# A tuned trunk kernel whose first projection block does without GpSimd's tensor arithmetic

## Chip, cores and metric

The kernel runs on one core of one Trainium2 chip. The metric is the device time of one launch in microseconds (us), of which the median of the runs is taken. The engines of the core are named as the profile names them: PE (TensorE, the matrix multiplier), DVE (VectorE), ACT (ScalarE), POOL (GpSimd) and SP (SyncE, which issues transfers). Every engine takes its instructions in the order in which they were written; engines wait for one another by semaphores.

## What is computed

The reference is a trunk of two layers on x (1 x 1024 x 1024, float32): a causal spatial-gating layer, then a Mamba-2 layer, each behind an RMSNorm. All that the change touches lies at the very start, in the norm and the first of three column groups of `h @ w_in`:

```python
def rmsnorm(x, w):
    xf = x.astype(jnp.float32)
    y = xf * lax.rsqrt(jnp.mean(xf * xf, axis=-1, keepdims=True) + NORM_EPS)
    return (y * w.astype(jnp.float32)).astype(x.dtype)

def spatial_gating_mixer(h, w_in, ln_w, ln_b, w_s, b_s, w_out):
    z, u, v = jnp.split(h @ w_in, 3, axis=-1)
    v = layernorm(v, ln_w, ln_b)
    ...
    return (u * mixed * jax.nn.silu(z)) @ w_out

h = h + spatial_gating_mixer(rmsnorm(h, norm_w), ...)
```

The columns of `v` are computed first, 512 at a time; `head()` computes the first 512 of them (block 0 of `v_block`), together with the norm and the transposes of x.

## The kernel before

**One block.** A block multiplies the normalized rows (1024 tokens x 1024) by 1024 x 512 weights. It cuts both into halves and uses seven products instead of eight. Of the rows, A11 and A12 are the first 512 tokens (first and second half of the contraction), A21 and A22 the other 512. Of the weights, b11, b12, b21, b22 are 512 x 256 each; they are loaded by SP into four slots `wr`. The sums are S1 = A21 + A22, S2 = S1 - A11, S3 = A11 - A21, S4 = A12 - S2 for the rows, and t1 = b12 - b11, t2 = b22 - t1, b21 - t2 and b22 - b12 for the weights. Product 1 takes A11, 2 takes A12, 3 takes S4, 4 takes A22, 5 takes S1, 6 takes S2, 7 takes S3.

**Two parts of each number.** Every operand is split into a rounded part and the rest (`hi` on ACT, then `lo` on DVE; names `hh`, `hl` for rows, `wh`, `wl` for weights). A product is then three matmuls: `wh*hh` (L134), `wl*hh` (L135), `wh*hl` (L136). One product is 48 matmuls of 128x256.

**The head's order.** `head()` is a schedule written out by hand. Rows come in eight tiles of 128 tokens, rows 0 to 3 for A11/A12, rows 4 to 7 for A21/A22. For each tile: the squares' sum (`sq`, ACT, L361), 1/sqrt in two parts (`rs_a`: DVE L365 and POOL's power L141; `rs_b`: four DVE operations on 128x2, L150 to L153), the scaling (`norm`, DVE, L376, two halves), eight transposes on PE (`tr`, L382), then copies back (`copy`, ACT, L398; the tile then holds the transposed row, F[t], in two halves) and the split (`hi` L391, `lo` L395). PE does products 1 and 2 half by half as rows come in, then 4 (with the transposes of rows 6 and 7 in between), 6, 7, 5, 3, and then product 1 of the next block (`nxt.mm(1)`).

**Who makes the sums.** POOL makes t1, t2 (L452, L453), b21 - t2 and b22 - b12 (L459, L460), S3 (L413), S1 of rows 4 to 6 (L416), the rest of two weights (`ylo`, L405) and S4 of rows 5 to 7 (L422). S4 needs A12 again, whose place was reused; `again` (L410) rebuilds it from its two parts. DVE makes S1 of row 7, S2 (L419) and S4 of row 4. In the trace the tile names are those of the program: `xp` holds rows 0 to 3, `xrow` rows 4 to 6, and row 7 lies in a slot `wr`, which it shares in turn with the weights; so `wr<-wr 128x512` is S1 of row 7. The junk output of the squares goes into the room of S4's split (`hh`, `hl`).

**The next block's weights** are loaded by SP (L120) into the same four `wr` slots, as each comes free. Stores of v go to `v_d` (L335).

Of the kernel before, what the change touches and what calls it, by code (L numbers as in the profile page):

```python
# [22 lines left out]
G = 8  # L23
# [6 lines left out]
def kernel(  # L30
# [49 lines left out]
    def wr(shape, name="wr"):  # L80
        return sb.tile(shape, F32, name=name, tag="wr", bufs=4)
# [90 lines left out]
    def new_H(names):  # L172
        return {n: (s8([P, 4, 512], "hh", F32R), s8([P, 4, 512], "hl", F32R)) for n in names}
# [3 lines left out]

    nwb = [k2([P, 512], "nwb") for _ in range(2)]
    xr = x.rearrange("(c p) d -> c p d", p=P)
    HS = new_H(("A11", "A12", "A22", "S1", "S2", "S3", "S4"))  # L180

    class Block:

# [103 lines left out]
        def post(self, n, i, parts=(0, 1)):  # L287
            a = self.acc[n][i]
            if n in (1, 6, 7) and 0 in parts:
                if i == 0:  # L290
                    self.u[n] = q4([P, 2, 512], "u")
                nc.scalar.copy(out=self.u[n][:, i], in_=a)  # L292
            if n == 2:
                self.done("C11", i, a, self.u[1][:, i])
            elif n == 4 and a is self.acc[1][i]:
                self.done("C21", i, a, None)
            elif n == 7 and 1 in parts and 4 in self.acc:
                self.done("C21", i, self.acc[4][i], self.u[7][:, i])
# [23 lines left out]
    def v_block(gp):  # L322
# [17 lines left out]

        return Block(HS, W, True, done)

    prow, prow2 = k1([P, P], "prow"), k1([P, P], "prow2")

    def head():

        blk = v_block(0)
        V, S, G = nc.vector, nc.scalar, nc.gpsimd
        TTv, TTg = V.tensor_tensor, G.tensor_tensor
        rows, F, TP, ss, rs = {}, {}, {}, {}, {}  # L350

        def load_x(t, dst):
            nc.sync.dma_start(out=dst, in_=xr[t])
            rows[t] = dst
            F[t] = dst.rearrange("p (h k t) -> p h k t", h=2, k=4)

        def sq(t):
            if t % 2 == 0:
                ss[t] = tiny([P, 8], "ss")
            junk = HS["S4"][t // 2 % 2][:, t % 2 * 2:t % 2 * 2 + 2].rearrange("p a b -> p (a b)")  # L360
            S.activation(junk, rows[t], AF.Square, accum_out=ss[t // 2 * 2][:, t % 2:t % 2 + 1])  # L361

        def rs_a(t):
            v = ss[t][:, 0:2]
            V.tensor_scalar(v, v, 1.0 / D, NORM_EPS, ALU.mult, ALU.add)  # L365
            ss[t + 1] = rsqrt_a(v, 2)

        def rs_b(t):
            r = tiny([P, 8], "rs")
            rsqrt_b(r[:, 0:2], ss[t][:, 0:2], ss[t + 1], 2)  # L370
            rs[t], rs[t + 1] = r[:, 0:1], r[:, 1:2]

        def norm(t):
            for kh in (0, 1) if t < 4 else (1, 0):
                xh = rows[t][:, kh * 512:(kh + 1) * 512]
                V.scalar_tensor_tensor(xh, xh, rs[t], nwb[kh], ALU.mult, ALU.mult)  # L376

        def tr(t):
            tp = [(sm if t in (0, 3, 5, 7) else acc)("tp") for _ in range(2)]
            for kh in (0, 1) if t < 4 else (1, 0):  # L380
                for k in range(4):
                    nc.tensor.transpose(out=tp[kh][:, k * P:(k + 1) * P],  # L382
                                        in_=rows[t][:, (kh * 4 + k) * P:(kh * 4 + k + 1) * P], identity=ident)
            TP[t] = [a.rearrange("p (k t) -> p k t", k=4) for a in tp]

        def part(name, t):
            sl = slice(t % 4 * P, (t % 4 + 1) * P)
            return [m[:, :, sl] for m in HS[name]]

        def hi(name, t, src):  # L390
            S.copy(out=part(name, t)[0], in_=src)  # L391

        def lo(name, t, src):
            h_, l_ = part(name, t)
            TTv(out=l_, in0=src, in1=h_.bitcast(F32), op=ALU.subtract)  # L395

        def copy(t, kh):
            S.copy(out=F[t][:, kh], in_=TP[t][kh])  # L398

        def yhi(n, src, eng=S.copy):  # L400
            blk.Y[n] = (wh([P, 4, 256]), wl([P, 4, 256]))
            eng(out=blk.Y[n][0], in_=src)
# [4 lines left out]
        def again(t):

            h_, l_ = part("A12", t)
            TTg(out=F[t][:, 1], in0=h_.bitcast(F32), in1=l_.bitcast(F32), op=ALU.add)  # L410

        def s3(t):
            TTg(out=F[t - 4][:, 0], in0=F[t - 4][:, 0], in1=F[t][:, 0], op=ALU.subtract)  # L413

        def s1(t, eng):
            eng(out=F[t][:, 0], in0=F[t][:, 0], in1=F[t][:, 1], op=ALU.add)  # L416

        def s2(t):
            TTv(out=F[t][:, 1], in0=F[t][:, 1], in1=F[t - 4][:, 0], op=ALU.subtract)  # L419

        def s4(t, eng=TTg):
            eng(out=F[t - 4][:, 1], in0=F[t - 4][:, 1], in1=F[t][:, 1], op=ALU.subtract)  # L422
# [11 lines left out]
        for kh, j in ((0, 0), (1, 0), (0, 1), (1, 1)):  # L434
            blk.load(kh, j)
        for t in range(4, 8):
            load_x(t, q4([P, D], "xrow") if t < 7 else wr([P, D]))

        nc.sync.dma_start(out=prow, in_=b_conv_w[0].rearrange("k (c p) -> (k c) p", p=P))
        for o, ap in ((0, a_ln_w), (16, a_ln_b), (32, b_norm_w), (48, b_conv_b)):  # L440
            n = ap.shape[1] // P
# [10 lines left out]
        TTg(out=t1, in0=b[0, 1], in1=b[0, 0], op=ALU.subtract)  # L452
# [28 lines left out]
        blk.mm(4, 1, False)
        yhi(7, b[0, 1]), ylo(7, b[0, 1], TTg)
        for t in (4, 5):
            s2(t), hi("S2", t, F[t][:, 1])
        for t in (4, 5):
            lo("S2", t, F[t][:, 1])
        s2(6), hi("S2", 6, F[6][:, 1]), s1(7, TTv), s2(7), hi("S2", 7, F[7][:, 1])
        for t in (6, 7):
            lo("S2", t, F[t][:, 1])
        for t in range(4):  # L490
            again(t)
# [8 lines left out]
        ylo(5, t1, TTg)  # L500
        s4(4, TTv)
        for t in range(5, 8):
            s4(t)
# [100 lines left out]
    for g in range(G):  # L604
# [41 lines left out]
        blk = Block(HS, lambda kh, j: [a_w_in[kh * 512:(kh + 1) * 512, j * DI + g * 256:j * DI + (g + 1) * 256]],  # L646
                    False, done_zu)
# [555 lines left out]
    V = nc.vector  # L1203
# [760 lines left out]
```

## Time and profile before

| | us |
|---|---|
| median of 3 runs (1590.07 to 1592.04) | 1591.79 |
| the profiled execution | 1599.45 |
| its span (first to last instruction) | 1597.6 |
| busy in the span: PE / DVE / ACT / POOL | 1503.3 / 1063.6 / 782.9 / 420.2 |
| granted TensorE clock, mean | 0.975 |

The span's 40 slices are 40 us each; in the first one PE is busy five tenths of the time, in the second seven tenths, and in nearly all others nine. The head is the first 92 us. A row of the timeline reads: start, duration, engine, line, operation, output and input tiles with their shape and type, count, and in brackets how long the engine stood idle ahead of it and for whom. A row with a count over 1 is a run of equal instructions with their total time.

### The profile page before, as it was taken

To read this page: it belongs to the slowest core of one execution; us is meant where nothing else is said; L and a number is where in the kernel's file an instruction comes from. 1 tells how busy PE (TensorE), PEld (TensorE's weight loads), DVE (VectorE), ACT (ScalarE), POOL (GpSimd) and SP (SyncE) were. 2 spreads that over 40 slices of the span, in tenths; PEclk is the share of its full clock that TensorE was granted. 3 is DMA by queue.
4 is the path that set the end of the run, shared out by engine and by line. 5 is a ranking of instruction groups with operands and counts; after the bars stand their busy time and mean duration, and the time that the engine had idled before them with its cause. 6 is when DMAs were issued, how large, how long until landed. Compare 5 with 4: busy or idle time off the path is not lost.

```text
span 1597.6 us, 21214 instructions
## 1 busy us (share of the span) xinstructions
PE 1503.3 (94%) x7830; PEld 1239.6 (78%) x7830; DVE 1063.6 (67%) x1701; ACT 782.9 (49%) x1251; POOL 420.2 (26%) x441
## 2 busy tenths in 40 slices
PE   5799999999999999998999999989999999987997
PEld 4799988888888887776788787767777777766876
DVE  7976566666666644777737377646776666777876
ACT  4522232332323354655555555546666666755363
POOL 3601110000000131210011312116766666532121
PEclk8899999999999999999999999999999999998999
DMA  5154323322333999856367878666566464677872
GB/s 174 41 174 143 106 98 111 111 98 98 110 110 111 329 262 245 191 128 139 99 159 178 165 165 158 162 188 188 162 180 179 133 183 126 198 270 167 221 139 105
DMA packets 174839, 251.82 MB, mean 158 GB/s; under 512 B 16288, under 2 KB 102928, under 8 KB 171536
## 3 DMA queue, kind: packets, MB, share of 16 engines
q1 hardware_dynamic: 124120, 168.39, 33.9%
q0 software_dynamic: 39520, 63.19, 20.5%
q10 hardware_dynamic: 11096, 18.90, 3.3%
q8 instruction: 62, 1.02, 0.3%
q14 instruction: 41, 0.34, 0.1%
HBM read 185.61 MB, written 51.18 MB: 148 GB/s over the span
## 4 chain that ended last, share of the span: by engine, by line
PE 59%; issue 15%; DVE 10%; ACT 7%; DMA 6%; POOL 1%; SPq 1%; ACTq 1%; POOLq 0%; DVEq 0%
PE acc L136 10%; PE acc L134 9%; PE acc L135 9%; PE ab L134 4%; PE ab L136 4%; PE ab L135 4%; PE yy L1571 2%; PE yy L1575 2%; DVE wl L112 2%; PE bo L135 2%; PE bo L134 2%; PE bo L136 2%; PE ao L134 2%; PE ao L135 2%; PE ao L136 2%
## 5 line engine op out<-in xcount | busy, mean ns | idle before, releaser
L134 PE MATMUL acc<-hh,wh 128*128 128x512 f32 x868 | 343.2, 395 | 15.0 <-ACT u L292 7.2
L136 PE MATMUL acc<-hh,wl 128*128 128x512 f32 x868 | 341.7, 394 | 2.2 <-DVE wl L112 2.1
L135 PE MATMUL acc<-hl,wh 128*128 128x512 f32 x868 | 340.2, 392 | 0.0
L134 PEld LDWEIGHTS acc<-hh,wh 128*128 128x128 f32 x868 | 164.6, 190 | 51.9 <-ACT u L292 8.9
L112 DVE TENSOR_TENSOR wl<-wr,wh 128x1024 fp32r<-128x1024 f32 (+1 forms) x97 | 115.6, 1193 | 125.8 <-ACT wh L111 125.8
L136 PEld LDWEIGHTS acc<-hh,wl 128*128 128x128 f32 x868 | 164.5, 189 | 39.9 <-DVE wl L112 5.5
L135 PEld LDWEIGHTS acc<-hl,wh 128*128 128x128 f32 x868 | 164.5, 190 | 33.4
L111 ACT CAST wh<-wr 128x1024 fp32r<-128x1024 f32 (+1 forms) x113 | 116.5, 1031 | 103.1 <-PE acc L135 56.7
L292 ACT COPY u<-acc 128x512 f32<-128x512 f32 x117 | 67.7, 583 | 200.1 <-PE acc L136 198.5
L136 PE MATMUL acc<-wh,hl 128*128 128x256 f32 x448 | 131.7, 294 | 12.4 <-DVE hl L395 12.4
L134 PE MATMUL ab<-hh,wh 128*128 128x512 f32 x288 | 129.5, 450 | 7.2 <-DVE x L1281 3.8
L134 PE MATMUL acc<-wh,hh 128*128 128x256 f32 x448 | 132.5, 296 | 3.8 <-DVE vt L331 2.1
L135 PE MATMUL acc<-wl,hh 128*128 128x256 f32 x448 | 130.9, 292 | 1.3 <-DVE wl L405 1.3
L135 PE MATMUL ab<-hl,wh 128*128 128x512 f32 x288 | 114.3, 397 | 3.2 <-DVE hl L112 3.2
L136 PE MATMUL ab<-hh,wl 128*128 128x512 f32 x288 | 115.2, 400 | 0.0
L136 PEld LDWEIGHTS acc<-wh,hl 128*128 128x128 f32 x448 | 90.2, 201 | 13.5 <-DVE hl L395 13.5
L134 PEld LDWEIGHTS acc<-wh,hh 128*128 128x128 f32 x448 | 90.4, 202 | 4.8 <-ACT wh L111 2.3
L135 PEld LDWEIGHTS acc<-wl,hh 128*128 128x128 f32 x448 | 90.5, 202 | 1.7 <-DVE wl L405 1.5
L134 PE MATMUL bo<-wh,xh 128*128 128x512 f32 x192 | 78.5, 409 | 8.0 <-ACT wh L111 7.2
L112 DVE TENSOR_TENSOR xl<-ya,xh 128x1024 fp32r<-128x1024 f32 x40 | 49.9, 1246 | 53.1 <-ACT xh L111 53.1
L1544 ACT ACTIVATE wl<-wl,tk 128x128 f32<-128x128 f32 x256 | 81.5, 391 | 0.6 <-DMA wl<-cs_d 0.3
L645 POOL DMA_DIRECT2D y_d<-y x8 | 4.4, 548 | 290.9 <-DVE y L642 290.9
(320 smaller groups left out, 3284.0 us busy)
## 6 DMA issues: line engine op xcount, KB each, us to landing
wr<-in_a_w_in_dram SPq DMA_DIRECT2D x48, 512.0 KB, 3.8
wl<-cs_d SPq DMA_DIRECT2D x64, 256.0 KB, 3.4
wr<-in_b_w_in_dram SPq DMA_DIRECT2D x30, 512.0 KB, 5.1
wb<-in_a_w_out_dram SPq DMA_DIRECT2D x10, 1024.0 KB, 11.2
wb<-in_b_w_out_dram SPq DMA_DIRECT2D x10, 1024.0 KB, 8.0
wr<-in_b_w_in_dram SPq DMA_DIRECT2D x36, 256.0 KB, 5.7
v<-v_d SPq DMA_DIRECT2D x8, 1024.0 KB, 5.0
y_d<-y POOLq DMA_DIRECT2D x8, 1024.0 KB, 5.6
```

Of the source, the lines that this page charges most:

```text
L111: nc.scalar.copy(out=hi, in_=src)
L112: return (eng or nc.vector).tensor_tensor(out=lo, in0=src, in1=hi.bitcast(F32), op=ALU.subtract)
L134: nc.tensor.matmul(out=o, lhsT=l[0], rhs=r[0], start=start, stop=False, **kw)
L135: nc.tensor.matmul(out=o, lhsT=l[0], rhs=r[1], start=False, stop=False, **kw)
L136: nc.tensor.matmul(out=o, lhsT=l[1], rhs=r[0], start=False, stop=stop, **kw)
L292: nc.scalar.copy(out=self.u[n][:, i], in_=a)
L645: store = lambda: nc.gpsimd.dma_start(out=y_d[-1], in_=y)
L1544: nc.scalar.activation(wl[:, j, :], wl[:, j, :], AF.Relu, scale=-1.0, bias=tokc(2, c, self.g)[:, j:j + 1])
L1571: nc.tensor.matmul(out=yy[f * 64:(f + 1) * 64, pt * P:(pt + 1) * P], lhsT=w[:, j * 64:(j + 1) * 64], rhs=wl[:, j, :], start=True, stop=True)
L1575: nc.tensor.matmul(out=yy[:, 256 + pt * P:384 + pt * P], lhsT=self.state[c - 1][:, pt * P:(pt + 1) * P], rhs=self.x(3, c), start=True, sto ...
```

## The change

POOL's tensor operations leave the head, except for the four tiny powers (L141); what they did goes to DVE, to ACT, or to transfers that add to their destination (`accum_op=ALU.add`).

- `copy` of rows 4 to 7 now multiplies by -1 (ACT), so the tiles hold -A21 and -A22, and every row sum becomes an addition: S3 = A11 + (-A21), -S1, -S2, and S4 = A12 + (-S2). `hi` and `lo` put the sign right for S1 and S2.
- The adds of S3 and S2, and of S1 for rows 6 and 7, are DVE's. S1 of rows 4 and 5 and all of S4 are adding transfers from tile to tile, issued by POOL.
- t1, t2 and b21 - t2 are DVE's. b22 - b12 is a multiplication by -1 on ACT and an adding transfer from memory (`add`, L202).
- A12 is kept by four more copies on ACT; `again` is gone. The rests of two weights (`ylo` 7 and 5) go from POOL to DVE.
- Row 7 goes into a `q4` tile like rows 4 to 6. The squares' junk and product 1's stored accumulator (`u[1]`) share a new tile `side`; the room of S4's split is taken only when it is needed.

```diff
         def hi(name, t, src):
-            S.copy(out=part(name, t)[0], in_=src)
+            h_ = part(name, t)[0]
+            if name in MINUS:
+                S.mul(h_, src, -1.0)
+            else:
+                S.copy(out=h_, in_=src)
...
         def copy(t, kh):
-            S.copy(out=F[t][:, kh], in_=TP[t][kh])
+
+            if t < 4:
+                S.copy(out=F[t][:, kh], in_=TP[t][kh])
+            else:
+                S.mul(F[t][:, kh], TP[t][kh], -1.0)
...
+        def sums(eng, *names):
+
+            for n, t in names:
+                a, c = {3: (F[t - 4][:, 0], F[t][:, 0]), 1: (F[t][:, 0], F[t][:, 1]),
+                        2: (F[t][:, 1], F[t - 4][:, 0]), 4: (F[t - 4][:, 1], F[t][:, 1])}[n]
+                if eng is None:
+                    nc.gpsimd.dma_start(out=a, in_=c, accum_op=ALU.add)
+                else:
+                    eng.tensor_tensor(out=a, in0=a, in1=c, op=ALU.add)
...
-            load_x(t, q4([P, D], "xrow") if t < 7 else wr([P, D]))
+            load_x(t, q4([P, D], "xrow"))
...
-        TTg(out=t1, in0=b[0, 1], in1=b[0, 0], op=ALU.subtract)
-        TTg(out=t2, in0=b[1, 1], in1=t1, op=ALU.subtract)
         blk.mm(1, 0, False), sq(4), blk.post(1, 0), sq(5)
         blk.mm(2, 0, False)
         norm(2), tr(2), norm(3), tr(3)
-        rs_a(4), rs_b(4), norm(4)
...
-        TTg(out=b[1, 0], in0=b[1, 0], in1=t2, op=ALU.subtract)
-        TTg(out=b[0, 1], in0=b[1, 1], in1=b[0, 1], op=ALU.subtract)
...
+        rs_a(4)
+        TTv(out=t1, in0=b[0, 1], in1=b[0, 0], op=ALU.subtract)
+        rs_b(4), norm(4)
...
         norm(5)
+        TTv(out=t2, in0=b[1, 1], in1=t1, op=ALU.subtract)
+        TTv(out=b[1, 0], in0=b[1, 0], in1=t2, op=ALU.subtract)
...
-        for t in (4, 5):
-            s3(t), s1(t, TTg)
-        yhi(6, t2)
+        sums(V, (3, 4), (3, 5)), sums(None, (1, 4), (1, 5))
+        S.mul(b[0, 1], b[0, 1], -1.0), blk.add(b[0, 1], 1, 1), yhi(6, t2)
...
-        s3(6), s1(6, TTg), s3(7)
+        sums(V, (2, 4), (2, 5), (3, 6), (1, 6))
         blk.mm(4, 1, False)
...
+            hi("S2", t, F[t][:, 1]), lo("S2", t, F[t][:, 1])
+        sums(V, (3, 7), (1, 7), (2, 7), (2, 6)), sums(None, (4, 4), (4, 5))
+        for t in (7, 6):
+            hi("S2", t, F[t][:, 1]), lo("S2", t, F[t][:, 1])
+        yhi(7, b[0, 1]), ylo(7, b[0, 1])
+        sums(None, (4, 6), (4, 7))
```

What this moves is seen best in the order of the instructions. First DVE between the squares of rows 4 and 5 and the rests of A11 and A12 of rows 2 and 3, before (L365 and L150 to L153 are the 1/sqrt, L376 the scaling, L395 the rests, L405 the rest of b21 - t2):

```order
L365 TENSOR_SCALAR ss<-ss 128x2
L150 TENSOR_TENSOR ru<-rr 128x2
L151 TENSOR_TENSOR ru<-ru,ss 128x2
L152 TENSOR_SCALAR ru<-ru 128x2
L153 TENSOR_TENSOR rs<-rr,ru 128x2
L376 SCALAR_TENSOR_TENSOR xrow<-xrow,rs,nwb 128x512 x2
L395 TENSOR_TENSOR hl<-tp,hh 128x4x128 x4
L376 SCALAR_TENSOR_TENSOR xrow<-xrow,rs,nwb 128x512 x2
L405 TENSOR_TENSOR wl<-wr,wh 128x1024
```

The same place in the changed kernel (`t_104` is t1, `t_105` is t2; the lines are 364, 375, 401 and 415 there, L598 is another part's tiny operation):

```order
L364 TENSOR_SCALAR ss<-ss 128x2
L461 TENSOR_TENSOR t_104<-wr 128x1024
L150 TENSOR_TENSOR ru<-rr 128x2
L151 TENSOR_TENSOR ru<-ru,ss 128x2
L152 TENSOR_SCALAR ru<-ru 128x2
L153 TENSOR_TENSOR rs<-rr,ru 128x2
L375 SCALAR_TENSOR_TENSOR xrow<-xrow,rs,nwb 128x512 x2
L401 TENSOR_TENSOR hl<-tp,hh 128x4x128 x4
L375 SCALAR_TENSOR_TENSOR xrow<-xrow,rs,nwb 128x512 x2
L467 TENSOR_TENSOR t_105<-wr,t_104 128x1024
L598 TENSOR_SCALAR hv<-hv 128x1
L468 TENSOR_TENSOR wr<-wr,t_105 128x1024
```

Three weight sums of 128x1024 came in: one between L364 and the 1/sqrt, two ahead of the rest of b21 - t2.

The second place is DVE at S2, the operand of product 6. Before (L405 the rest of t2, L395 the rests, L419 the S2 of rows 4, 5, 6 and 7, `wr<-wr` S1 of row 7):

```order
L405 TENSOR_TENSOR wl<-t_107,wh 128x1024
L395 TENSOR_TENSOR hl<-tp,hh 128x4x128 [waits PE_49,Activation_49]
L419 TENSOR_TENSOR xrow<-xrow,xp 128x512 [waits Pool_49] x2
L395 TENSOR_TENSOR hl<-xrow,hh 128x4x128 [waits Activation_49] x2
L419 TENSOR_TENSOR xrow<-xrow,xp 128x512 [waits Pool_49]
L416 TENSOR_TENSOR wr<-wr 128x512 [waits PE_49,Pool_49]
L419 TENSOR_TENSOR wr<-wr,xp 128x512 [waits DVE_49]
```

In the changed kernel (`xrow<-xrow,xp` is S2, `xp<-xp,xrow` S3, `xrow<-xrow` S1; a name that begins with DMASW is the semaphore of a POOL queue transfer):

```order
L415 TENSOR_TENSOR wl<-t_105,wh 128x1024
L401 TENSOR_TENSOR hl<-tp,hh 128x4x128 [waits PE_49,Activation_49]
L425 TENSOR_TENSOR xrow<-xrow,xp 128x512 [waits DMASW0_49]
L425 TENSOR_TENSOR xrow<-xrow,xp 128x512 [waits DMASW1_49]
L425 TENSOR_TENSOR xp<-xp,xrow 128x512
L425 TENSOR_TENSOR xrow<-xrow 128x512 [waits DVE_49]
L399 SCALAR_TENSOR_TENSOR hl<-xrow,hh 128x4x128 [waits Activation_49] x2
L425 TENSOR_TENSOR xp<-xp,xrow 128x512
L425 TENSOR_TENSOR xrow<-xrow 128x512 [waits DVE_49,PE_49]
```

S2 of rows 4 and 5 waited for POOL's S3 and S1; now it waits for the adding transfers of S1, which read the same half that S2 then overwrites, and S3 and S1 of row 6 stand behind it.

The third place is POOL's queue after the last power (L423 the adding transfers: `xrow<-xrow` S1 of rows 4 and 5, `xp<-xrow` S4; L202 adds b22 to -b12; L335 stores v):

```order
L423 DMA xrow<-xrow 128x512 [waits DMAHW2_49,DVE_49,Activation_49]
L423 DMA xrow<-xrow 128x512 [waits DMAHW3_49,DVE_49]
L202 DMA wr<-in_a_w_in_dram 128x4x256 [waits Activation_49]
L423 DMA xp<-xrow 128x512 [waits DMAHW0_49,DVE_49]
L423 DMA xp<-xrow 128x512 [waits DMAHW1_49,DVE_49]
L423 DMA xp<-xrow 128x512 [waits DMAHW4_49,DVE_49]
L423 DMA xp<-xrow 128x512 [waits DMAHW5_49]
L335 DMA v_d_93<-vt 128x512 [waits DVE_49]
```

In this stretch POOL held 16 tensor operations before; now it only issues seven adding transfers. From the first product of the next block on, the order is the same on every engine.

More of the change, by code (lines that the diff above doesn't have):

```diff
@@ L179 @@
     xr = x.rearrange("(c p) d -> c p d", p=P)
-    HS = new_H(("A11", "A12", "A22", "S1", "S2", "S3", "S4"))
+    HS = new_H(("A11", "A12", "A22", "S1", "S2", "S3"))
     class Block:
@@ L289, in post @@
             if n in (1, 6, 7) and 0 in parts:
-                if i == 0:
+                if i == 0 and n not in self.u:
                     self.u[n] = q4([P, 2, 512], "u")
@@ L347, in head @@
         blk = v_block(0)
-        V, S, G = nc.vector, nc.scalar, nc.gpsimd
-        TTv, TTg = V.tensor_tensor, G.tensor_tensor
+        V, S = nc.vector, nc.scalar
+        TTv, MINUS = V.tensor_tensor, ("S1", "S2")
         rows, F, TP, ss, rs = {}, {}, {}, {}, {}
@@ L359, in sq @@
                 ss[t] = tiny([P, 8], "ss")
-            junk = HS["S4"][t // 2 % 2][:, t % 2 * 2:t % 2 * 2 + 2].rearrange("p a b -> p (a b)")
-            S.activation(junk, rows[t], AF.Square, accum_out=ss[t // 2 * 2][:, t % 2:t % 2 + 1])
+            S.activation(side[:, 0], rows[t], AF.Square, accum_out=ss[t // 2 * 2][:, t % 2:t % 2 + 1])
         def rs_a(t):
@@ L390, in hi @@
         def hi(name, t, src):
-            S.copy(out=part(name, t)[0], in_=src)
+            h_ = part(name, t)[0]
[3 more added lines that the diff above has]
+                S.copy(out=h_, in_=src)
         def lo(name, t, src):
             h_, l_ = part(name, t)
-            TTv(out=l_, in0=src, in1=h_.bitcast(F32), op=ALU.subtract)
+            if name in MINUS:
+                V.scalar_tensor_tensor(l_, src, -1.0, h_.bitcast(F32), ALU.mult, ALU.subtract)
+            else:
+                TTv(out=l_, in0=src, in1=h_.bitcast(F32), op=ALU.subtract)
         def copy(t, kh):
-            S.copy(out=F[t][:, kh], in_=TP[t][kh])
+            if t < 4:
+                S.copy(out=F[t][:, kh], in_=TP[t][kh])
+            else:
+                S.mul(F[t][:, kh], TP[t][kh], -1.0)
         def yhi(n, src, eng=S.copy):
@@ L405, in ylo @@
             eng(out=blk.Y[n][1], in0=src, in1=blk.Y[n][0].bitcast(F32), op=ALU.subtract)
[L407 to L422, printed above, removed]
+        def sums(eng, *names):
[4 more added lines that the diff above has]
+                    nc.gpsimd.dma_start(out=a, in_=c, accum_op=ALU.add)
+                else:
+                    eng.tensor_tensor(out=a, in0=a, in1=c, op=ALU.add)
         b = blk.b
@@ L426, in head @@
         blk.t1, blk.t2 = t1, t2
+        side = s8([P, 2, 1024], "side")
+        blk.u[1] = side[:, 1].rearrange("p (i n) -> p i n", i=2)
         xp = [s8([P, 2, D], "xp") for _ in range(2)]
@@ L445, in head @@
         norm(0), tr(0), norm(1), tr(1)
-        hi("A11", 0, TP[0][0]), copy(0, 0), sq(3), hi("A12", 0, TP[0][1])
+        hi("A11", 0, TP[0][0]), copy(0, 0), sq(3), hi("A12", 0, TP[0][1]), copy(0, 1)
         rs_a(2), yhi(1, b[0, 0], V.tensor_copy)
         lo("A11", 0, TP[0][0]), ylo(1, b[0, 0]), lo("A12", 0, TP[0][1]), rs_b(2)
-        hi("A11", 1, TP[1][0]), copy(1, 0), hi("A12", 1, TP[1][1])
+        hi("A11", 1, TP[1][0]), copy(1, 0), hi("A12", 1, TP[1][1]), copy(1, 1)
         lo("A11", 1, TP[1][0]), lo("A12", 1, TP[1][1])
         yhi(2, b[1, 0]), ylo(2, b[1, 0])
-        TTg(out=t1, in0=b[0, 1], in1=b[0, 0], op=ALU.subtract)
-        TTg(out=t2, in0=b[1, 1], in1=t1, op=ALU.subtract)
         blk.mm(1, 0, False), sq(4), blk.post(1, 0), sq(5)
@@ L456, in head @@
         norm(2), tr(2), norm(3), tr(3)
-        rs_a(4), rs_b(4), norm(4)
-        hi("A11", 2, TP[2][0]), copy(2, 0), hi("A12", 2, TP[2][1])
-        TTg(out=b[1, 0], in0=b[1, 0], in1=t2, op=ALU.subtract)
-        TTg(out=b[0, 1], in0=b[1, 1], in1=b[0, 1], op=ALU.subtract)
-        lo("A11", 2, TP[2][0]), lo("A12", 2, TP[2][1])
-        hi("A11", 3, TP[3][0]), copy(3, 0), hi("A12", 3, TP[3][1])
-        lo("A11", 3, TP[3][0]), lo("A12", 3, TP[3][1])
+        rs_a(4)
+        TTv(out=t1, in0=b[0, 1], in1=b[0, 0], op=ALU.subtract)
+        rs_b(4), norm(4)
+        for t in (2, 3):
+            hi("A11", t, TP[t][0]), copy(t, 0), hi("A12", t, TP[t][1]), copy(t, 1)
+            lo("A11", t, TP[t][0]), lo("A12", t, TP[t][1])
         norm(5)
+        TTv(out=t2, in0=b[1, 1], in1=t1, op=ALU.subtract)
+        TTv(out=b[1, 0], in0=b[1, 0], in1=t2, op=ALU.subtract)
         blk.mm(1, 1, False, (0,)), tr(4), blk.mm(1, 1, False, (1,))
@@ L479, in head @@
         lo("A22", 7, TP[7][1])
-        s3(6), s1(6, TTg), s3(7)
+        sums(V, (2, 4), (2, 5), (3, 6), (1, 6))
         blk.mm(4, 1, False)
-        yhi(7, b[0, 1]), ylo(7, b[0, 1], TTg)
         for t in (4, 5):
[L484 to L491, printed above, removed]
+            hi("S2", t, F[t][:, 1]), lo("S2", t, F[t][:, 1])
[4 more added lines that the diff above has]
+        sums(None, (4, 6), (4, 7))
         for i in range(2):
@@ L499, in head @@
             lo("S3", t, F[t - 4][:, 0])
[L500 to L503, printed above, removed]
+        ylo(5, t1)
         for i in range(2):
@@ L516, in head @@
             nxt.load(kh, j)
+        HS.update(new_H(("S4",)))
         for t in range(4, 8):
```

## Prediction

> **What bounds the kernel now.** The page's slices point at the first 90 us, so I read stretches of it first (columns: length, busy time of PE, its weight loads, DVE, ACT and POOL, granted clock, DMA share, GB/s).
>
> ```profile
> 20.00:60.00 40.00, 27.48 (x182) 26.49 (x182) 37.01 (x47) 18.47 (x36) 21.06 (x15) 0.83 0.18 50
> 60.00:92.00 32.00, 27.77 (x190) 27.40 (x191) 29.42 (x36) 13.61 (x22) 12.34 (x7) 0.84 0.22 77
> 92.00:112.00 20.00, 20.00 (x169) 20.00 (x168) 14.10 (x20) 6.23 (x8) 1.34 (x2) 1.00 0.74 222
> ```
>
> From 20 to 60 us DVE works 37 of 40 us and everybody waits for it. From 92 us PE never stops: a head that ends earlier hands its gain to PE whole. So the head's end, the first matmul of the next block's product 1 at 92.08, is what to move. PE's timeline shows the waits on the way:
>
> ```profile
> 22.13 0.58 PE L136 MATMUL acc<-wh,hl 128*128 128x256 f32 x1 [3.13 <-DVE hl L395]
> 34.49 0.58 PE L136 MATMUL acc<-wh,hl 128*128 128x256 f32 x1 [3.85 <-DVE hl L395]
> 47.70 1.94 PE L382 MATMUL tp<-ident,xrow 128*128 128x128 f32 x8 [2.97 <-issue]
> 60.36 0.39 PE L136 MATMUL acc<-wh,hl 128*128 128x256 f32 x1 [3.28 <-DVE hl L395]
> 66.76 0.39 PE L136 MATMUL acc<-wh,hl 128*128 128x256 f32 x1 [1.74 <-DVE hl L395]
> 84.77 0.36 PE L134 MATMUL acc<-wh,hh 128*128 128x256 f32 x1 [2.12 <-DVE vt L331]
> 92.08 0.28 PE L134 MATMUL acc<-wh,hh 128*128 128x256 f32 x1
> ```
>
> Nearly all name DVE's rests. A wait also costs clock, as the same view of shorter stretches shows:
>
> ```profile
> 68.10:71.30 3.20, 3.20 (x17) 3.20 (x17) 2.79 (x5) 1.70 (x5) 0.00 (x0) 0.50 0.00 0
> 85.20:88.40 3.20, 3.20 (x17) 3.20 (x16) 3.17 (x6) 0.00 (x0) 0.00 (x0) 0.50 0.50 187
> 88.80:92.00 3.20, 3.20 (x29) 3.20 (x28) 3.17 (x7) 0.00 (x0) 0.00 (x0) 1.00 0.44 164
> ```
>
> After the waits at 66.76 and 84.77 the granted clock is 0.50 for a while: 17 matmuls in 3.2 us where there are 29 at full clock. Such a stretch loses 12/29 of 3.2, and with its edges about 1.4 us.
>
> Why is DVE late? Its timeline beside POOL's:
>
> ```profile
> 7.96 0.16 DVE L150 TENSOR_TENSOR ru<-rr 128x2 f32<-128x2 f32 x1 [0.83 <-POOL rr L141]
> 8.76 2.74 DVE L376 SCALAR_TENSOR_TENSOR xp<-xp,rs,nwb 128x512 f32<-128x512 f32 x4
> 16.44 2.37 POOL L452 TENSOR_TENSOR t<-wr 128x1024 f32<-128x1024 f32 x1 [1.36 <-DMA wr<-in_a_w_in_dram]
> 16.77 2.06 DVE L150 TENSOR_TENSOR ru<-rr 128x2 f32<-128x2 f32 x1
> 21.38 1.29 DVE L395 TENSOR_TENSOR hl<-tp,hh 128x512 fp32r<-128x512 f32 x2
> 27.34 2.33 DVE L150 TENSOR_TENSOR ru<-rr 128x2 f32<-128x2 f32 x1 [0.81 <-POOL rr L141]
> 32.42 1.42 DVE L376 SCALAR_TENSOR_TENSOR xrow<-xrow,rs,nwb 128x512 f32<-128x512 f32 x2
> ```
>
> An operation on 128x2 takes 0.16 us at 7.96 and 2.06 at 16.77, ending at 18.83, just when POOL's L452 ends (18.81). I read it so that a POOL tensor operation holds such a DVE operation until it is done. This is what the change takes away.
>
> **The change part by part.** The sum follows the chain to 92.08.
>
> *Up to 22.13.* The four operations of the 1/sqrt take 0.80 us (7.96 to 8.76) when POOL is idle, and 4.61 here (16.77 to 21.38): 3.8 less. Two more copies on ACT (0.6 each) now stand ahead of the halves that DVE reads here; I keep **3.5**.
>
> *22.13 to 34.49.* The same four go from 5.08 (27.34 to 32.42) to 0.8: 4.3 less. Among them now stands the sum t1 on DVE. Its price:
>
> ```profile
> 96.62 1.22 DVE L260 TENSOR_TENSOR wr<-wr 128x1024 f32<-128x1024 f32 x1
> 97.76 1.21 DVE L225 TENSOR_TENSOR wr<-wr,t 128x1024 f32<-128x1024 f32 x1
> ```
>
> One after the other they cost 1.14 each, of which 0.81 falls into the idle time ahead of 27.34. Net **4.0**.
>
> *34.49 to 47.70.* Here the change costs: two more sums on DVE (2.3) now stand ahead of ACT's rounding of b21 - t2, and behind that, on ACT, stand two halves of row 4 and the squares of rows 6 and 7. The prices on ACT and the places on DVE:
>
> ```profile
> 43.37 1.08 ACT L402 CAST wh<-t 128x1024 fp32r<-128x1024 f32 x1
> 39.72 1.06 ACT L361 ACTIVATE hl<-wr 128x1024 fp32r<-128x1024 f32 x1
> 40.90 0.17 DVE L365 TENSOR_SCALAR ss<-ss 128x2 f32<-128x2 f32 x1 [1.39 <-ACT hl L361]
> 42.37 0.77 DVE L150 TENSOR_TENSOR ru<-rr 128x2 f32<-128x2 f32 x1
> 45.65 0.68 DVE L395 TENSOR_TENSOR hl<-tp,hh 128x512 fp32r<-128x512 f32 x1
> 46.25 2.00 DVE L376 SCALAR_TENSOR_TENSOR xrow<-xrow,rs,nwb 128x512 f32<-128x512 f32 x2
> ```
>
> With 7.5 gained, DVE comes to the rests of rows 2 and 3 at 26.2 (32.42 and 1.3 for two scalings, less 7.5). From there: four rests 2.6, two scalings 1.4, two sums 2.3, ACT's rounding 1.1, two halves 1.2 and two squares of 1.2 with their readout bring the next L365 to 37.2, against 40.90 before: only 3.7 of the 7.5 are left there. From there on it wins again: the four tiny operations take 3.28 (42.37 to 45.65) and will take 0.8, two scalings 2.00 against 1.42.
>
> 3.7 + 2.5 + 0.6 = 6.8, so the term is **-0.7**: row 6's transposes move from 47.70 to about 40.9.
>
> *47.70 to 60.36, the new wait.* DVE's S2:
>
> ```profile
> 54.71 3.92 DVE L419 TENSOR_TENSOR xrow<-xrow,xp 128x512 f32<-128x512 f32 x2
> 58.56 3.44 DVE L395 TENSOR_TENSOR hl<-xrow,hh 128x512 fp32r<-128x512 f32 x2
> 61.93 1.76 DVE L419 TENSOR_TENSOR xrow<-xrow,xp 128x512 f32<-128x512 f32 x1
> 63.61 1.76 DVE L416 TENSOR_TENSOR wr<-wr 128x512 f32<-128x512 f32 x1
> ```
>
> Undisturbed one costs 0.65 (the two rests at 21.38). The two S2 save 2.7, the first rest 1.1, the rest of t2 ahead of them another 1.1. Added: S3 of rows 4 and 5 (1.2), and S3 and S1 of row 6 ahead of the rests (1.3). What is left hangs on the S1 transfers of 256 KB, which POOL issues when S3 of rows 4 and 5 and the scaled halves are there, at about 43.7 and 44.5. No transfer of before is one from tile to tile at this place. The nearest are L745's adding ones:
>
> ```profile
> ya<-ya POOLq DMA_DIRECT2D x12, 512.0 KB, 15.4
> L745 POOL DMA_DIRECT2D u<-h_d x1: 865/865/865, 1497.7 to 1497.7; - x1
> DMA to landing us min/median/max: 5.0/5.0/5.0
> DMA to landing us min/median/max: 4.5/11.0/23.5
> ```
>
> The second and third rows are one 256 KB transfer that was first in its queue, 5.0 us; the last row is all of L745, 4.5 to 23.5, most of them queued behind others. Here POOL's queue is empty, so I take 5.0, with the second 1.5 later: 48.7 and 50.2. DVE reaches S2 at about 47.9, so it stands 0.8 and then some 0.9. Sum: -4.9 + 2.5 + 1.7 = **0.7** gained; both ends of the landing (4.5 and 23.5) are kept for the range.
>
> The Trainium skill, "DMA: Bandwidth & Descriptors", section "Anatomy of one DMA — SWDGE (gpsimd) path", fits 2.0 us plus the bytes at 436 GB/s; by it 256 KB would land in an estimated 2.6 us, DVE would not wait, and some 1.5 us more would be gained. The lone row says 5.0 and decides.
>
> *60.36 to 66.76.* Three operations of 1.76 (the rest, S2 and S1) become 0.6 each, but one S3 comes in: the rests of rows 6 and 7 are done 1.5 sooner than this stretch took: **1.5**.
>
> *66.76 to 84.77.* DVE's rests of S1, and with them product 5 and the accumulator at 84.77:
>
> ```profile
> 72.90 5.88 DVE L395 TENSOR_TENSOR hl<-xrow,hh 128x512 fp32r<-128x512 f32 x3 [2.01 <-ACT hh L391]
> 78.70 1.78 DVE L395 TENSOR_TENSOR hl<-wr,hh 128x512 fp32r<-128x512 f32 x1
> ```
>
> Four rests take 7.66 beside POOL, and 2.6 without it; against these 5.1 stand two rests of weights (2.3) that come to DVE, while one S4 add (0.7) leaves. DVE gets some 3.5 us of air, and the wait of 2.12 at 84.77 goes; next late would be the S4 transfers, issued by about 57 and needed at about 69. With PE fed after 66.8, the slow matmuls of 68 to 71 go as well (1.4): **3.5**.
>
> *84.77 to 92.08.* No wait, so no slow stretch from 85.2: **1.4**.
>
> At nothing: ACT's multiplication by -1 costs what a copy costs (two rows below, 627 and 595 ns), and ACT is busy only 18.5 of the 40 us from 20 on. Row 7's load, the squares' place and S4's room free nothing that a wait names. SP's next weights go out earlier, since a `wr` slot is free; beside the S1 transfers two of them may cost up to 3 us, which the range takes in.
>
> ```profile
> L217 ACT ACTIVATE t<-wr 128x512 f32<-128x512 f32 x1 | 0.6, 627 | 0.0
> L398 ACT COPY xrow<-tp 128x512 f32<-128x512 f32 x6 | 3.3, 595 | 0.0
> ```
>
> **Sum:** 3.5 + 4.0 - 0.7 + 0.7 + 1.5 + 3.5 + 1.4 = 13.9 us: 92.08 becomes 78.2, and the profiled 1599.45 (its span of 1597.6 and 1.85 around it, which nothing touches) becomes 1585.5. The profiled execution is 7.7 longer than the median 1591.79; the head is a fixed piece of both, so the median becomes **1577.9**.
>
> **Rivals.**
>
> *The transfers land late.* For it: all of L745 have a median of 11.0, and two SP loads run beside. Each microsecond over 5.0 holds S2 and all DVE work behind it as long. 7 to 12 us cost 2 to 7: 1580 to 1585.
>
> The Trainium skill, "SBUF — State Buffer", section "SBUF: two separate sides", says that such transfers starve while DVE runs an operation that uses both of its ports, since POOL can't write their descriptors. By it they would land only in DVE's pauses, which the first S2 would make itself. POOL's issue of the lone row, 865 ns, shows no such stall, but not with DVE at work as densely as here.
>
> *The waits come back.* DVE has seven operations more between 42 and 70 us (four S3, one S1, two rests of weights); if the waits at 66.76 and 84.77 stay with their slow stretches, 3.5 and 1.4 fall away: 13.9 - 4.9 = 9.0, so 1582.8.
>
> *Slower.* The transfers take what `ya<-ya` takes, median 15.4. With a landing of L, S2 is L - 5.0 later, and so are the last S4 adds, issued at 57 + (L - 5.0) and landing L + 1.3 after that: at 53.3 + 2L. Product 3 needs them; its 48 matmuls (5.3 to 5.8 us at full clock, by 29 in 3.2 and a few lost records) and a slow stretch (1.4) put the next block at 60.5 + 2L. It decides from L = 15.8 (92.08); with 20 the head ends at 100.5, 8.4 late: 1592 to 1600. Against it: those rows are twice as large and stand in a queue of their own kind.
>
> *It doesn't do what it says:* DVE's long operations are not POOL's doing. Then DVE keeps them and carries some 8 us of added work (three sums and two rests of weights at 1.14, five row sums at 0.65, less one S4): slower, 1592 to 1600. Against it stand the common ends at 18.8.
>
> **How the numbers follow.** A measurement tells about 0.2% (3 us) from no change. Forecast 0.76 (1574.5 to 1580.5: slow stretches ±1.4, latencies ±0.7, a landing of 4.5 to 6), late transfers 0.12, waits back 0.06, slower 0.03, POOL not the cause 0.03. The range 1573.5 to 1585 takes in the first three. A partial loss that ends within 3 us of before is about 0.03, cut from the second and third: faster 0.91, same 0.03, slower 0.06.
>
> **What would show it.** Tiny operations of 0.16 us at 17 and 24 us; row 6's transposes near 41; DVE waiting for a transfer ahead of the first S2 at about 48, under 1.5 us; no wait of PE for `vt` near 72; the next block's L134 at 78 ± 3. Wrong it would be if the S1 rows show landings over 10 us, or if PE of the next block, which now starts earlier, waits for its weights.

## The result and the profile after

| | before | after |
|---|---|---|
| median, us | 1591.91 (4 runs, 1590.07 to 1596.3) | 1581.48 (4 runs, 1579.54 to 1582.27) |
| the profiled execution, its span | 1599.45, 1597.6 | 1582.27, 1580.5 |
| head's end (first matmul of the next block) | 92.08 | 78.42 |

The medians are 10.4 us apart. The ratio of the runs is 0.9929 (11.3 us) with a 95% interval of 0.9906 to 0.9951, so the gain lies between 7.8 and 15.0 us. The forecast was 1577.9, 13.9 us faster.

The stretches of the changed kernel (columns as before: length, busy PE, weight loads, DVE, ACT, POOL, clock, DMA share, GB/s):

```profile
20.00:60.00 40.00, 29.45 (x214) 28.05 (x214) 32.93 (x58) 22.91 (x44) 9.03 (x9) 0.91 0.49 102
60.00:92.00 32.00, 32.00 (x269) 32.00 (x269) 29.74 (x47) 14.96 (x23) 1.15 (x2) 1.00 0.51 159
```

From 60 us on PE never stops, at full clock; POOL's 9 us up to 60 are mostly the issuing of transfers. DVE is busy for 33 us instead of 37 between 20 and 60 though it does eleven operations more. PE's timeline, with the waits that are left:

```profile
27.03 0.38 PE L136 MATMUL acc<-wh,hl 128*128 128x256 f32 x1 [1.59 <-DVE hl L401]
40.38 1.94 PE L381 MATMUL tp<-ident,xrow 128*128 128x128 f32 x8 [3.20 <-ACT wr L477]
53.69 0.58 PE L136 MATMUL acc<-wh,hl 128*128 128x256 f32 x1 [3.44 <-DVE hl L399]
78.42 0.28 PE L134 MATMUL acc<-wh,hh 128*128 128x256 f32 x1
```

DVE's timeline at the places of the prediction:

```profile
16.52 0.15 DVE L150 TENSOR_TENSOR ru<-rr 128x2 f32<-128x2 f32 x1
17.18 1.29 DVE L401 TENSOR_TENSOR hl<-tp,hh 128x512 fp32r<-128x512 f32 x2
24.16 0.16 DVE L150 TENSOR_TENSOR ru<-rr 128x2 f32<-128x2 f32 x1 [0.59 <-POOL rr L141]
24.96 1.41 DVE L375 SCALAR_TENSOR_TENSOR xrow<-xrow,rs,nwb 128x512 f32<-128x512 f32 x2
36.80 0.17 DVE L364 TENSOR_SCALAR ss<-ss 128x2 f32<-128x2 f32 x1 [1.38 <-ACT side L360]
48.34 0.69 DVE L425 TENSOR_TENSOR xrow<-xrow,xp 128x512 f32<-128x512 f32 x1 [1.16 <-DMA xrow<-xrow]
51.01 0.69 DVE L425 TENSOR_TENSOR xrow<-xrow,xp 128x512 f32<-128x512 f32 x1 [1.98 <-DMA xrow<-xrow]
```

The 1/sqrt takes 0.66 us (16.52 to 17.18) and 0.80 (24.16 to 24.96), instead of 4.61 and 5.08. The next L364 comes at 36.80 (forecast 37.2). The new wait is there: 1.16 and 1.98 us ahead of the two S2. The two transfers for which it waits, by their line:

```profile
L423 POOL DMA_DIRECT2D xrow<-xrow x2: 1046/1139/1232, 43.5 to 44.2; - x2
DMA to landing us min/median/max: 4.8/5.8/6.8
```

### The profile page after: what moved, and what is told of

Read it like the earlier page. It is cut to its first block, busy times and chain, and to the rows that moved or that the text cites. A ratio compares the mean times of both kernels' runs of the same rounds, so it can differ in the third digit from the quotient of the medians.

```text
span 1580.5 us, 21221 instructions
## 1 busy us (share of the span) xinstructions
PE 1495.9 (95%) x7830; PEld 1232.2 (78%) x7830; DVE 1047.2 (66%) x1710; ACT 785.9 (50%) x1256; POOL 392.4 (25%) x428
## 4 chain that ended last, share of the span: by engine, by line
PE 60%; issue 15%; DVE 11%; ACT 8%; DMA 5%; POOL 1%; ACTq 0%; SPq 0%; POOLq 0%; DVEq 0%
PE acc L136 10%; PE acc L134 10%; PE acc L135 10%; PE ab L134 4%; PE ab L136 4%; PE ab L135 4%; PE yy L1569 2%; PE yy L1573 2%; DVE wl L112 2%; PE ao L134 2%; PE ao L135 2%; PE ao L136 2%; ACT wh L111 2%; PE bo L135 2%; PE bo L134 2%
## 5 line engine op out<-in xcount | busy, mean ns | idle before, releaser
L134 PE MATMUL ao<-wh,xh 128*128 128x512 f32 x192 | 76.3, 397 | 3.6 <-ACT u L853 3.6
## 6 DMA issues: line engine op xcount, KB each, us to landing
wb<-in_a_w_out_dram SPq DMA_DIRECT2D x10, 1024.0 KB, 12.2
```

Of the source, the lines that this page charges most:

```text
L134: nc.tensor.matmul(out=o, lhsT=l[0], rhs=r[0], start=start, stop=False, **kw)
```

## The experiments

Each variant was profiled once, the changed kernel twice and the kernel before three times. A single time does not separate what differs by 3 us: behind the head's end, where the code is the same, the spans of all these profiles have between 1496.3 and 1505.5 us left, in no relation to the edit. So the head's end is what is compared; it was 78.4 us in the changed kernel. The head does not start at quite the same instant either: the first product's first matmul stands between 14.05 and 15.09 us (14.41 in the changed kernel), and a difference of a few tenths at the head's end can come from there.

### The kernels themselves, again

> The kernel before, unchanged, profiled once more. If the head decides, its end (first matmul of the next block's product 1) is again at 92.1 +-0.3 us, while the rest behind it, 1505.5 us in the first profile, may differ by some us between executions; then the 17 us between the two profiled spans are 13.7 of head and 3 of chance. Rival: the rest is 1505.5 +-0.5 again, and the changed kernel's 1502.1 is an effect of the change.

> The kernel before, a third profile. Its head ended at 92.1 us once, with PE waiting 2.1 us for vt and two stretches of half clock, and at 88.9 us once, without. If 92.1 was the exception, it ends at 89 +-1 without the wait; if it is the rule, at 92 with it.

> The changed kernel, a second profile: the head's end again at 78.4 +-0.5, since no wait of it stands near a tipping point behind 54 us; the rest behind the head differs by a few us as it did for the kernel before.

The changed kernel's head ended at 78.28, as expected. The kernel before gave three values: 92.08, 88.91 and 90.73, and 1505.5, 1499.2 and 1502.4 us behind them; the changed kernel has 1502.1 and 1502.5 there. First e1's lines (two stretches, then PE):

```profile
67.00:72.00 5.00, 5.00 (x44) 5.00 (x43) 3.90 (x6) 4.63 (x9) 1.27 (x1) 1.00 0.00 0
85.00:89.00 4.00, 4.00 (x35) 4.00 (x35) 3.93 (x9) 0.00 (x0) 0.00 (x0) 1.00 0.35 131
```

```profile
83.09 0.35 PE L134 MATMUL acc<-wh,hh 128*128 128x256 f32 x1 [2.50 <-DVE vt L331]
88.91 0.28 PE L134 MATMUL acc<-wh,hh 128*128 128x256 f32 x1
```

And of e10:

```profile
67.00:72.00 5.00, 5.00 (x43) 5.00 (x43) 3.81 (x7) 4.63 (x9) 0.71 (x1) 1.00 0.00 0
85.00:89.00 4.00, 4.00 (x30) 4.00 (x29) 3.93 (x8) 0.00 (x0) 0.00 (x0) 0.81 0.40 150
```

```profile
83.64 0.55 PE L134 MATMUL acc<-wh,hh 128*128 128x256 f32 x1 [2.48 <-DVE vt L331]
90.73 0.28 PE L134 MATMUL acc<-wh,hh 128*128 128x256 f32 x1
```

So the wait for `vt` (2.1 to 2.5) is there each time; e10's expectation had taken e1 for a run without it, and its 90.73 lies between the two values that it named. What comes and goes is mainly the stretch at half clock behind a wait: the first profile had one at 68 to 71 and one from 85, e10 only the second (from `vt` to the head's end 7.1 us instead of 5.8), e1 neither. The other 0.6 of the 3.2 us between e1 and the first profile were there at the first matmul (14.05 against 14.67). By the mean of the three (90.6), the head gained 12.2 us, and between 10.5 and 13.8 by the single ones. The measured 10.4, with its interval of 7.8 to 15.0, agrees with that. The part behind the head was 3 us shorter in the first pair of profiles; that lies within what the kernel before shows by itself.

### Does a POOL operation hold DVE?

One operation more on POOL (e6):

```diff
         rs_a(2), yhi(1, b[0, 0], V.tensor_copy)
+        nc.gpsimd.tensor_tensor(out=t2, in0=b[0, 1], in1=b[0, 0], op=ALU.subtract)
```

> Changed kernel with one POOL tensor operation of 128x1024 more, b12 - b11 into t2's room (written again later), which nothing waits for in time; it runs from about 16.4 to 18.8 us. Theory (POOL holds DVE): the 1/sqrt of rows 2 and 3 takes 2.7 instead of 0.7 us, its held operation ends with POOL's, and the head ends about 2 us later (80.5). Rival (only waits on POOL's results made DVE late): the 1/sqrt stays at 0.7 us and the head ends at 78.4.

POOL's and DVE's timelines, and PE's at the head's end:

```profile
16.84 2.38 POOL L453 TENSOR_TENSOR t<-wr 128x1024 f32<-128x1024 f32 x1 [1.33 <-DMA wr<-in_a_w_in_dram]
17.19 2.05 DVE L150 TENSOR_TENSOR ru<-rr 128x2 f32<-128x2 f32 x1
19.75 1.29 DVE L401 TENSOR_TENSOR hl<-tp,hh 128x512 fp32r<-128x512 f32 x2
81.47 0.28 PE L134 MATMUL acc<-wh,hh 128*128 128x256 f32 x1
```

DVE's L150 has nothing to do with that POOL operation's tiles; it ends at 19.24, and POOL's at 19.22. The 1/sqrt takes 2.56. The head ends 3.05 later, of which 0.67 was there at the start already (17.19 against 16.52). The rival falls: a POOL operation beside DVE is enough to make DVE late.

Not every DVE operation is held, though. In the kernel before, a rest that reads one operand (`tp`) from the memory into which PE writes its results took its usual 0.68 in the middle of a POOL operation. A rest that reads neither operand from there (`hl<-xrow,hh`) took 1.7 and more beside POOL, as the prediction's rows at 58.56 and 72.90 show:

```profile
53.85 1.47 POOL L413 TENSOR_TENSOR xp<-xp,wr 128x512 f32<-128x512 f32 x1 [0.74 <-ACT wr L398]
54.11 0.68 DVE L395 TENSOR_TENSOR hl<-tp,hh 128x512 fp32r<-128x512 f32 x1
```

The weight sums back on POOL (e2):

```diff
-        TTv(out=t1, in0=b[0, 1], in1=b[0, 0], op=ALU.subtract)
-        TTv(out=t2, in0=b[1, 1], in1=t1, op=ALU.subtract)
-        TTv(out=b[1, 0], in0=b[1, 0], in1=t2, op=ALU.subtract)
+        nc.gpsimd.tensor_tensor(out=t1, in0=b[0, 1], in1=b[0, 0], op=ALU.subtract)
+        nc.gpsimd.tensor_tensor(out=t2, in0=b[1, 1], in1=t1, op=ALU.subtract)
         blk.mm(1, 0, False), sq(4), blk.post(1, 0), sq(5)
...
         rs_b(4), norm(4)
+        nc.gpsimd.tensor_tensor(out=b[1, 0], in0=b[1, 0], in1=t2, op=ALU.subtract)
```

> Changed kernel with t1, t2 and b21 - t2 back on POOL at their old places. Theory (a POOL tensor operation holds DVE's two-operand operations): the 1/sqrt of rows 2 and 3 is back at 4.6 us instead of 0.7, that of rows 4 and 5 at about 5 instead of 0.8; PE's waits at 22 and 34 us return; DVE is spared 3.4 us, row 6's transposes move from 40.4 to about 44.5 and the head's end from 78.4 to about 82.5; time about 1585.5. Rival (DVE's long operations had another cause): they stay short, DVE is spared three sums, the head ends 1 to 3 us sooner.

```profile
16.25 2.03 DVE L150 TENSOR_TENSOR ru<-rr 128x2 f32<-128x2 f32 x1
18.51 2.21 DVE L152 TENSOR_SCALAR ru<-ru 128x2 f32<-128x2 f32 x1
26.80 2.32 DVE L150 TENSOR_TENSOR ru<-rr 128x2 f32<-128x2 f32 x1 [0.81 <-POOL rr L141]
```

```profile
31.82 0.39 PE L136 MATMUL acc<-wh,hl 128*128 128x256 f32 x1 [1.20 <-DVE hl L401]
40.86 1.27 PE L381 MATMUL tp<-ident,xrow 128*128 128x128 f32 x8
78.57 0.28 PE L134 MATMUL acc<-wh,hh 128*128 128x256 f32 x1
```

The holds are back, and PE is 4.8 us later at the second wait (31.82 against 27.03), but at row 6's transposes only 0.5 later, and at the head's end nothing is left. A miss of both expectations (82.5, or 1 to 3 sooner): what holds cost up to 32 us, DVE's three sums ahead of ACT's chain cost in the next stage. That chain begins with the rounding of b21 - t2, here in the changed kernel, after a wait for the last sum, and then in e2, without one:

```profile
32.52 1.05 ACT L412 CAST wh<-wr 128x1024 fp32r<-128x1024 f32 x1 [4.49 <-DVE wr L468]
32.93 1.13 ACT L412 CAST wh<-wr 128x1024 fp32r<-128x1024 f32 x1
```

### What the other parts are worth

Rests of two weights back on POOL (e4; in both calls of `ylo` for products 7 and 5, `TTg` is given as the engine):

> Changed kernel with the rests of two weights (products 7 and 5) back on POOL. Theory (POOL's operations hold DVE's rests here too, but there is slack behind 60 us): the four rests of S3 and the four of S1 take 4 to 5 us each instead of 2.5, PE doesn't wait, the head's end stays at 78.4 +-0.5. Rival (these two were what the stretch from 66 us on hung on): PE waits for vt again and the head ends 2 to 5 us later.

```profile
62.82 2.41 POOL L417 TENSOR_TENSOR wl<-t,wh 128x1024 fp32r<-128x1024 f32 x1 [0.61 <-ACT wh L412]
```

```profile
63.29 4.29 DVE L399 SCALAR_TENSOR_TENSOR hl<-xrow,hh 128x512 fp32r<-128x512 f32 x4 [0.41 <-ACT hh L392]
```

The four rests of S1 take 4.29 instead of 2.5, those of S3 3.49, and the head ends at 78.26: there is slack, as expected.

Row 7 back in a slot of the weights (e7), and the same with the weight sums on POOL as well (e9):

```diff
-            load_x(t, q4([P, D], "xrow"))
+            load_x(t, q4([P, D], "xrow") if t < 7 else wr([P, D]))
```

> Changed kernel with row 7 back in a slot of the weights, so that the next block's first loads of 512 KB can't start at 45 us. Theory (the S1 transfers land late because SP's loads run beside them): the second S1 transfer lands after about 5.5 us instead of 6.8, DVE's waits at S2 shrink by about 1 us and the head ends at about 77.4. Rival (they wait for one another and for DVE alone): 6.8 us again, and 78.4.

> Changed kernel with t1, t2 and b21 - t2 on POOL and row 7 in a slot of the weights, both as before; what is left of the change is the row sums, b22 - b12 and the two rests of weights off POOL, and the kept A12. Theory (the weight sums and row 7's place gain nothing by themselves; the place only pays for t1 on DVE, which holds that slot longer): row 7's load starts at about 18.8 us again, and the head ends at 78.5 +-1. Rival (row 7's own place is worth a few us in any case): row 6's transposes stay above 43 us and the head ends at 80 to 85.

SP, ACT and PE of e7:

```profile
23.53 0.70 SPq L353 DMA_DIRECT2D wr<-in_x_dram  x1
```

```profile
42.29 1.06 ACT L360 ACTIVATE side<-wr 128x1024 f32<-128x1024 f32 x1 [6.74 <-DMA wr<-in_x_dram]
```

```profile
84.94 0.28 PE L134 MATMUL acc<-wh,hh 128*128 128x256 f32 x1
```

This one missed altogether: the head ends 6.5 us later, not 1 us sooner. The slot is read by t1, which DVE makes at 22 to 24 us; so row 7's load is issued at 23.53, behind the loads of the second layer's small vectors, and ACT, by the trace, waits for it until 42.29. In e9, with t1 on POOL, it is issued at 18.70, ahead of those, and the head ends at 79.79:

```profile
79.79 0.28 PE L134 MATMUL acc<-wh,hh 128*128 128x256 f32 x1
```

So e9 carries 10.8 of the 12.2 us (from 90.6): the row sums, b22 - b12 and the kept A12 bring nearly all of the gain (the two rests of weights, off POOL here too, bring nothing by e4). Row 7's place brings at most 1.2 on top (e9 to e2; 0.4 of it stood there at the first matmul, 14.53 against 14.15), and it is what makes t1 on DVE bearable.

Where e9 gains can be read as far as row 6's transposes:

```profile
29.70 2.28 DVE L151 TENSOR_TENSOR ru<-ru,ss 128x2 f32<-128x2 f32 x1
42.52 0.41 PE L381 MATMUL tp<-ident,xrow 128*128 128x128 f32 x2
```

The second row is e9's: 5.2 sooner than 47.70. The first is of the kernel before, an operation held by POOL's b22 - b12; without that it takes 2.1 less. The four tiny operations at 42.37 take 0.65 in e9 instead of 3.28, and two scalings 0.6 less: 5.3 together. That is a sum of rows; which of the row sums weighs most was not tried one by one.

### The new wait

S1 of rows 4 and 5 on DVE (e3):

```diff
-        sums(V, (3, 4), (3, 5)), sums(None, (1, 4), (1, 5))
+        sums(V, (3, 4), (3, 5)), sums(V, (1, 4), (1, 5))
```

> Changed kernel with S1 of rows 4 and 5 as two adds on DVE instead of two adding transfers. Theory (S2 waits for the landings): DVE's idle times of 1.2 and 2.0 us ahead of S2 vanish, two adds (1.3) come in; PE's wait that ends at 53.7 ends at about 51.9, the head at about 76.6 instead of 78.4. Rival (DVE's own work sets the pace there): the head ends up to 1.3 us later.

```profile
47.88 1.28 DVE L425 TENSOR_TENSOR xrow<-xrow,xp 128x512 f32<-128x512 f32 x2
```

```profile
51.15 0.39 PE L136 MATMUL acc<-wh,hl 128*128 128x256 f32 x1 [1.37 <-DVE hl L399]
75.88 0.28 PE L134 MATMUL acc<-wh,hh 128*128 128x256 f32 x1
```

S2 follows without a wait, and the head ends 2.5 us sooner (0.3 of it stood there at the first matmul, 14.10), though DVE does two adds more.

The squares of rows 6 and 7 earlier on ACT (e5):

```diff
+        sq(6), sq(7)
         norm(5)
...
-        yhi(4, b[1, 0]), hi("A22", 4, TP[4][1]), copy(4, 1), sq(6), sq(7)
+        yhi(4, b[1, 0]), hi("A22", 4, TP[4][1]), copy(4, 1)
```

> Changed kernel with the squares of rows 6 and 7 issued on ACT right behind the copies of row 3 (ACT is idle there from 28 to 32 us) instead of behind the rounding of b21 - t2. Theory (the third stage hangs on ACT's chain behind b21 - t2): row 6's transposes move from 40.4 to about 39.0, the head's end from 78.4 to about 77.0; time about 1580. Rival (the S1 transfers or the weight sums set the pace there): no change within 0.3 us of the head's end.

```profile
38.92 1.48 PE L381 MATMUL tp<-ident,xrow 128*128 128x128 f32 x8 [1.93 <-DVE xrow L375]
49.91 0.38 PE L134 MATMUL acc<-wh,hh 128*128 128x256 f32 x1 [2.63 <-ACT hh L392]
77.92 0.28 PE L134 MATMUL acc<-wh,hh 128*128 128x256 f32 x1
```

Row 6's transposes come 1.5 sooner, as expected, but at 49.91 PE waits 2.63 where it waited 1.06: 0.5 of the 1.5 arrives. The S1 transfers were issued at 42.06 and 42.80 and took 6.4 and 7.7 us instead of 4.8 and 6.8, so the first landed no sooner and the second 0.5 sooner (48.5 and 50.5, against 48.3 and 51.0).

Both together (e8):

> Changed kernel with both: squares of rows 6 and 7 early on ACT, S1 of rows 4 and 5 on DVE. Theory: early squares alone moved row 6's transposes by 1.5 us but the head by 0.5 only, as the S1 transfers landed no sooner; with both, PE's wait of 53.7 ends at about 50.5 and the head at about 75.3, 3 us sooner; time about 1578.5. Rival (a later wait takes over): the head ends at 77 to 78.

```profile
50.20 0.39 PE L136 MATMUL acc<-wh,hl 128*128 128x256 f32 x1 [1.37 <-DVE hl L399]
74.92 0.28 PE L134 MATMUL acc<-wh,hh 128*128 128x256 f32 x1
```

The head ends 3.5 us sooner than in the changed kernel. The median is 1578.76 (6 runs, 1575.43 to 1580.56) against 1592.53 of the kernel before (11 runs), ratio 0.9911 (0.9895 to 0.9928). It is the best of the kernels by the head's end; its interval overlaps with the change's.

## Why the prediction was right, and where its sizes were off

The chain was walked from the first profile, and against that profile each of its points came out within 0.8 us, as the instants of the same matmuls show (us gained up to there):

| instant before | forecast | measured |
|---|---|---|
| 22.13 | 3.5 | 3.2 |
| 34.49 | 7.5 | 7.5 |
| 47.70 | 6.8 | 7.3 |
| 60.36 | 7.5 | 6.7 |
| 66.76 | 9.0 | 8.4 |
| 84.77 | 12.5 | 12.1 |
| 92.08 | 13.9 | 13.7 |

That the last line agrees to 0.2 us is partly luck: the stage of the new wait was 1.3 too good, and the other six terms together 1.1 too low. The median of 1581.48 lies inside the range, but 1 us above the band of the forecast proper (1574.5 to 1580.5). By its time it falls among the late transfers, yet not by their mechanism, which had landings of 7 to 12 us where 4.8 and 6.8 were measured.

- *POOL holds DVE's operations*: shown by e6, and by e2's return of 2.03, 2.21 and 2.32 us.
- *34.49 to 47.70, the weight sums cost*: right in sign, but 0.2 where 0.7 was forecast. Of the 7.5 gained ahead of it, 4.8 come from moving the three sums (e2 against the changed kernel), but they are no gain of the head: e2 leaves the sums on POOL and ends at the same instant (78.57). The prediction had the cost of the move in the next stage and did not see that it takes back all that the move brings.
- *The new wait*: 0.8 and 0.9 us were forecast, 1.16 and 1.98 measured. The first landing (5.0 taken, 4.8 measured) was right; the second came 2.7 us behind the first (at 51.0 against 48.3), not 1.5. So the stage lost 0.6 where the prediction's sum (in costs there, -0.7) gave 0.7 gained: this is its mis-sized term. e3 shows that the wait cost 2.5 at the head's end, with its two adds paid.
- *The waits at 66.76 and 84.77 go*: right. But one step made the forecast too good: that the profiled head is "a fixed piece" of the median run as well. It holds the two terms on the clock, 1.4 for the stretch at 68 to 71 and 1.4 for that from 85, read from one execution as if each wait of that size brought one; of three, one had the first and two the second, in full or nearly. By these shares an ordinary run could gain about half of the 2.8. The base of 92.08 was the longest of three, 1.5 over their mean of 90.6, and the gain from that mean is 12.2. Between 12.2 and the 10.4 of the medians another 1.8 are left; they lie within the interval, and no run here says what they are.
- *Slower, by landings over 15.8 us*: no S1 or S4 transfer took more than 10.2 us in any of the runs.

The Trainium skill, "SBUF — State Buffer", section "SBUF: two separate sides", would have POOL's transfers starve while DVE runs an operation in a two-port mode, and the prediction's rival took DVE's work here for such. The changed kernel does not decide this, since its first S1 transfer landed (48.3) when DVE already stood idle. In e7 the first S1 transfer was issued at 50.1 and landed after 3.6 us, while DVE worked without a pause up to 53.8 and went on with S2 unhindered:

```profile
L423 POOL DMA_DIRECT2D xrow<-xrow x1: 1043/1043/1043, 50.1 to 50.1; - x1
DMA to landing us min/median/max: 3.6/3.6/3.6
```

So no such stall shows with the operations that DVE runs here. What makes the first landing 3.6 in one run and 6.4 in another stays open: e7 was meant to try SP's loads beside them, but its edit moved the whole stage; so no run shows what such loads cost, for which the prediction's range took in up to 3 us.

## What to carry over

A POOL tensor operation can hold a DVE operation until it ends, also where no data connects the two: 1.90 us more for DVE in e6, where 2.03 of POOL's operation were left when DVE's began, and 1.80 for 1.94 in e4. Look for operations on two columns that take 2 us. Yet undo each part of a change before giving it credit: here the terms of the chain added up, and still two of the parts that they were put down to (the weight sums, the rests of two weights) brought nothing. And a term for a slowed clock behind a wait wants more than one execution, since it is there in some and not in others.

## What was not expected of the hardware

- Of two adding transfers of 256 KB, issued 0.7 us apart on POOL, the second landed 2.7 us after the first in the changed kernel. The 512 KB one of L202, issued 0.55 us behind them, took 12.5 us (10.6 to 12.9 in the runs). Standing behind them is not the reason: in e3 and e8, without the S1 transfers, it took 10.6 and 12.6. What makes it slow stays open.
- The hold goes the other way too: in the changed kernel POOL's power took 1.60 us when it began beside DVE's t1 (22.53, in DVE's 22.36 to 23.58), and 0.71 at 7.32, with DVE idle.
- A 512 KB load of a row, issued behind small loads in the same queue (e7), held ACT until 18.8 us after its issue. The trace shows no landing for it, but in its stretches (the last two columns are the DMA share and GB/s) the bytes come no sooner either:

```profile
24.00:36.00 12.00, 9.57 (x80) 9.16 (x79) 10.05 (x17) 7.17 (x14) 0.06 (x1) 1.00 0.05 0
38.00:40.00 2.00, 0.00 (x0) 0.00 (x0) 0.00 (x0) 0.00 (x0) 0.00 (x0) 1.00 0.32 96
40.00:42.00 2.00, 0.00 (x0) 0.00 (x0) 0.00 (x0) 0.00 (x0) 0.00 (x0) 0.81 0.61 214
```

  For 12 us the core's 16 DMA engines move next to nothing, at a busy share of 0.05, which is less than one engine's. The changed kernel and e9 have the same share there, with no large load behind. That fits one engine at work on the small loads ahead; which of them is to blame was not tried. In e9, issued ahead of them, the row landed after 4.2 us and held nobody.
- Behind the head, the same instructions took 1496.3 to 1505.5 us.
